# Pinned short products of the ones matrix in TensorE's waits of the norm chains

## The chip, the cores and the metric

The kernel runs on one core of one Trainium2 chip. The metric is the device time of one execution in microseconds (us); the median of several runs is given. Beside it there is one profiled execution, whose trace gives a start and a duration for each instruction on TensorE (PE; its weight loads stand apart as PEld), VectorE (DVE), ScalarE (ACT), GpSimd (POOL) and the DMA queues, and the clock that TensorE was granted, as a share of full speed.

## The reference

One inference step of a two-layer backbone on 256 tokens of width 2048: 128 context tokens and 128 latent tokens share all weights. Every layer is a mixer (layer 0: differential attention beside RWKV-7; layer 1: a Conformer convolution) followed by a gated MLP. Ahead of each of the four blocks stands an RMS norm with adaptive scale and shift; inside the Conformer block there is a layer norm besides.

```python
def rmsnorm(x, g, eps=RMS_EPS):
    xf = x.astype(F32)
    y = xf * lax.rsqrt(jnp.mean(xf * xf, axis=-1, keepdims=True) + eps)
    return (y * g.astype(F32)).astype(x.dtype)
...
    for l in range(DEPTH):
        ...
        hs = rmsnorm(xs, norm_g[l, 0]) * (1.0 + sc1s) + sh1s
        # layer 0: ms = ab_mixer(hs, ...)     layer 1: ms = conformer_conv(hs, ...)
        xs = xs + g1s * ms
        hs = rmsnorm(xs, norm_g[l, 1]) * (1.0 + sc2s) + sh2s
        xs = xs + g2s * conv_ffn(hs, w_up[l], w_ffn_dw[l], w_down[l])
...
def conformer_conv(h, w_pw1, w_dw, b_dw, cln_g, cln_b, w_pw2):
    u = h @ w_pw1
    u = u[..., :D_CONV] * jax.nn.sigmoid(u[..., D_CONV:])
    u = dwconv(u, w_dw) + b_dw
    u = jax.nn.silu(layernorm(u, cln_g, cln_b))
    return u @ w_pw2
```

The six adaptive vectors of a layer (`sc1`, `sh1`, `g1`, `sc2`, `sh2`, `g2`) come from a product of SiLU of the conditioning with a 2048 x 12288 matrix, `w_ada`. All data is float32.

## The kernel before

Activations lie transposed: channels on the 128 partitions, the 256 tokens (two streams of 128) along the free axis, in 16 slices of the width, called kt. A large product (`gemm`) runs over kt and makes three matmuls of 128x256 for each output tile, on values split into a rounded high part and a remainder: high by high (L252), high by low (L254), low by high (L255). Weights come from HBM into `raw` tiles (seven of them), ACT rounds them (L192), DVE or POOL takes the remainder (L194), into four `wbt` buffers. With `tail=4` the last four kt of a product run tile by tile (L268 to L270), so that the tiles of the last group end one after the other. The residual and its squares follow each tile on DVE and ACT (L666, L509, L511).

Between two stages stands a norm chain. `rstd_tok` makes the sums of squares of each token with four products of the collected squares with two columns of `ones` (L522); `rstd` takes the root on ACT (L528) and the reciprocal on DVE (L529); `rstd_bcast` puts the two results on a diagonal (`dg`, L534 on ACT and L535 on DVE) and multiplies it with `ones` (L537), which lays the factor on all partitions in PSUM. Then `modulated` makes the next stage's input kt by kt: DVE multiplies (L582), ACT adds the shift and rounds (L585), DVE takes the remainder (L587), and the next product begins with the first kt. This chain runs three times with its sums made on TensorE: ahead of layer 0's MLP, ahead of the Conformer block, ahead of layer 1's MLP. The first norm of all has its sums from ACT and isn't touched; the final one ends the program.

The layer norm of the Conformer block has a chain of its own: sums by products with two columns of `ones` (L1711), a few small DVE and ACT operations (L1715 to L1723), four diagonals (L1728, L1730), one product of 128x512 with `ones` (L1733), and then `hc` kt by kt (L1737 to L541), which the second Conformer product takes.

The products for `w_ada` are spread over the program as fill: `ada_pe` makes them on TensorE (L421), `ada_vec` makes them on DVE (L446) and ends with eight short products (L454). Both collect in one PSUM tile with the tag `ada`, of which there is a single buffer; DVE turns the result round when a part is done (L460) and adds the bias (L473).

The order on each engine is set by a scheduler, which simulates the program's time line and takes the ready instruction of highest priority; `tc.high_priority` raises it. `tc.keep_in_program_order` pins an instruction to its place among the others that are pinned. The engines themselves run their queues in order.

In the program's text the sums, the diagonal and its product of an RMS norm stand in one place, in `modulated`:

```python
with tc.high_priority(0):
    rs = acc if known else rstd_bcast(rstd_tok(acc))
```

The products that the change adds read the constant tile `ones` twice and write the PSUM tile with the tag `ada`:

```python
psa = ctx.enter_context(tc.tile_pool(name="psa", bufs=1, space=PSUM))
ones = const.tile([P, P], F32, name="ones")
```

Of the kernel before, what the change touches and what calls it, by code (L numbers as in the profile page):

```python
# [10 lines left out]
F32 = mybir.dt.float32  # L11
# [8 lines left out]
P = 128  # L20
# [62 lines left out]
def tile_step(ctx: ExitStack, tc: tile.TileContext, A):  # L83
# [42 lines left out]
    def bank():  # L126
        return psm[0].tile([P, 512], F32, tag="mm", name="mm")
# [21 lines left out]
    def new_hb():  # L149
        return Halves([hbp.tile([P, KT // 2, 2 * TT], F32R, tag="hb", name="hbt") for _ in range(2)])  # L150
# [366 lines left out]
    def rstd_tok(acc):  # L517

        ps = bank()
        for s in range(2):  # L520
            for i, src in enumerate((acc, sq_last[0])):
                pe.matmul(ps[:, 2 * s:2 * s + 2], lhsT=src[:, s * T:(s + 1) * T], rhs=ones[:, 0:2], start=(i == 0),  # L522
                          stop=(i == 1))
        return rstd(ps[:, 0:4])
# [7 lines left out]
    def rstd_bcast(sd):  # L532
        dg = nrm_[0].tile([P, TT], F32, tag="dg", name="dg")
        act.activation(dg[:, T:TT], ident, AF.Copy, scale=sd[:, 2:3])  # L534
        dve.tensor_scalar(out=dg[:, 0:T], in0=ident, scalar1=sd[:, 0:1], scalar2=None, op0=ALU.mult)  # L535
        rs = bank()
        pe.matmul(rs[:, 0:TT], lhsT=ones, rhs=dg, start=True, stop=True)  # L537
        return rs

    def split(dst, src, eng=None):  # L540
        act.activation(dst[:, 0:TT], src, AF.Copy)  # L541
        (eng or dve).tensor_tensor(out=dst[:, TT:2 * TT], in0=src, in1=dst[:, 0:TT].bitcast(F32), op=ALU.subtract)
# [19 lines left out]
    def modulated(x, acc, l, ni, known=False, in_psum=False):  # L562
        sh = "sh1" if ni == 0 else "sh2"

        def gen(hb):
            with tc.high_priority(0):
                rs = acc if known else rstd_bcast(rstd_tok(acc))
            pair = [None]
            for kt in range(KT):
                if not in_psum:  # L570
# [887 lines left out]
    with ExitStack():  # L1458
# [55 lines left out]
        with scoped("nrm1", 2) as nrm_[0]:  # L1514
# [76 lines left out]
            with scoped("cv", 1) as cvp, scoped("cvt", 2) as cvt:  # L1591
# [134 lines left out]
                for i in range(4):  # L1726
                    if i % 2:
                        act.activation(dg[:, i], ident, AF.Copy, scale=va[:, 2 * i:2 * i + 1])  # L1728
                    else:
                        dve.tensor_scalar(out=dg[:, i], in0=ident, scalar1=va[:, 2 * i:2 * i + 1], scalar2=None,  # L1730
                                          op0=ALU.mult)
                pbc = bank()
                pe.matmul(pbc, lhsT=ones, rhs=dg.rearrange("p a t -> p (a t)"), start=True, stop=True)  # L1733
                hc = new_hb()
                for ct in range(KT):
                    t = cvt.tile([P, TT], F32, tag="cg", name="cg")
# [79 lines left out]
```

## Time and profile before

| | |
|---|---|
| median of 3 runs | 2710.97 us (2711.49, 2710.97, 2693.57) |
| the profiled execution | 2685.66 us |
| its span, first to last instruction | 2683.7 us |
| mean granted clock of TensorE | 0.982 |
| PE busy | 2590.8 us, 97% of the span |
| DVE busy | 2010.5 us, 75% |
| ACT busy | 1258.9 us, 47% |

The profile's time axis starts with the first instruction. The stages that matter here: layer 0's mixer ends near 807 us, its MLP runs to 1565, the first half of the Conformer block to 1835, its second half to 1949, and layer 1's MLP to the end. In a row of the time line stand the start and the duration in us, the engine, the line of the kernel, the operation, the tiles written and read, how many alike were merged (x), and in brackets the idle time before it with what ended it. A product of float32 operands is carried out as two matmul instructions, so that x2 is one product of the program. In a row of a table of stretches stand the stretch, its length, each engine's busy time with the number of instructions in brackets, the granted clock (PEclk), the share of DMA time and GB/s.

### The profile page before, as it was taken

To read this page: it belongs to the slowest core of one execution; us is meant where nothing else is said; L and a number is where in the kernel's file an instruction comes from. 1 tells how busy PE (TensorE), PEld (TensorE's weight loads), DVE (VectorE), ACT (ScalarE), POOL (GpSimd) and SP (SyncE) were. 2 spreads that over 40 slices of the span, in tenths; PEclk is the share of its full clock that TensorE was granted. 3 is DMA by queue.
4 is the path that set the end of the run, shared out by engine and by line. 5 is a ranking of instruction groups with operands and counts; after the bars stand their busy time and mean duration, and the time that the engine had idled before them with its cause. 6 is when DMAs were issued, how large, how long until landed. Compare 5 with 4: busy or idle time off the path is not lost.

```text
span 2683.7 us, 60347 instructions
## 1 busy us (share of the span) xinstructions
PE 2590.8 (97%) x24347; PEld 2429.0 (91%) x24347; DVE 2010.5 (75%) x3442; ACT 1258.9 (47%) x2063; POOL 310.7 (12%) x333
## 2 busy tenths in 40 slices
PE   6999998999998999999999989999999999999998
PEld 5898995677998999999999979977989999999998
DVE  3667755766579899888999978985389985566655
ACT  4335544545345444434444454345355453355544
POOL 2000111011100000000000038763300000000000
PEclk9999999999798999999999999999999999999999
DMA  9986666656366888877878857876878876666653
GB/s 301 351 286 191 191 181 238 224 182 222 111 193 190 250 261 256 277 247 249 275 251 265 273 161 229 287 256 205 290 235 278 270 233 194 196 193 193 195 191 118
DMA packets 421368, 616.58 MB, mean 230 GB/s; under 512 B 32437, under 2 KB 291864, under 8 KB 420448
## 3 DMA queue, kind: packets, MB, share of 16 engines
q1 hardware_dynamic: 416688, 600.83, 70.4%
q0 software_dynamic: 3040, 6.57, 0.7%
q10 hardware_dynamic: 1360, 5.33, 0.5%
q8 instruction: 191, 3.13, 0.5%
q14 instruction: 89, 0.73, 0.1%
HBM read 604.75 MB, written 7.86 MB: 228 GB/s over the span
## 4 chain that ended last, share of the span: by engine, by line
PE 83%; DVE 4%; DMA 2%; ACT 1%; issue 1%; SPq 0%; POOL 0%; DVEq 0%; ACTq 0%; POOLq 0%
PE mm L252 23%; PE mm L255 23%; PE mm L254 23%; PE ada L421 3%; DMA raw<-in_w_ada 1%; PE mm L1088 1%; DMA raw<-in_w_up 1%; DVE wbt L194 1%; PE mm L1649 1%; PE mm L1121 1%; PE mm L1125 0%; DVE av L446 0%; PE ada L454 0%; PE mm L1283 0%; PE mm L1292 0%
## 5 line engine op out<-in xcount | busy, mean ns | idle before, releaser
L192 ACT ACTIVATE wbt<-raw 128x1024 fp32r<-128x1024 f32 (+3 forms) x768 | 795.3, 1037 | 1033.1 <-PE mm L254 698.1
L252 PE MATMUL mm<-hbt,wbt 128*128 128x256 f32 x3888 | 1085.0, 282 | 8.5 <-ACT hbt L585 6.4
L194 DVE TENSOR_TENSOR wbt<-raw,wbt 128x1024 fp32r<-128x1024 f32 (+1 forms) x688 | 814.1, 1189 | 359.7 <-ACT wbt L192 349.9
L254 PE MATMUL mm<-hbt,wbt 128*128 128x256 f32 x3888 | 1080.7, 280 | 2.2 <-DVE hbt L587 2.1
L255 PE MATMUL mm<-hbt,wbt 128*128 128x256 f32 x3888 | 1063.1, 280 | 7.5 <-DVE wbt L194 5.4
L252 PEld LDWEIGHTS mm<-hbt,wbt 128*128 128x128 f32 x3888 | 732.7, 189 | 26.5 <-issue 12.5
L254 PEld LDWEIGHTS mm<-hbt,wbt 128*128 128x128 f32 x3888 | 733.8, 189 | 5.9 <-DVE hbt L587 4.4
L255 PEld LDWEIGHTS mm<-hbt,wbt 128*128 128x128 f32 x3888 | 723.3, 189 | 12.3 <-DVE wbt L194 6.7
L254 PE MATMUL mm<-u,wbt 128*128 128x256 f32 x1344 | 371.0, 278 | 0.0
L252 PE MATMUL mm<-u,wbt 128*128 128x256 f32 x1344 | 370.9, 278 | 0.0
L255 PE MATMUL mm<-u,wbt 128*128 128x256 f32 x1344 | 365.7, 278 | 0.0
L446 DVE SCALAR_TENSOR_TENSOR av<-raw,silu_c,av 128x1024 f32<-128x1024 f32 x270 | 337.6, 1279 | 35.3 <-DMA raw<-in_w_ada 35.0
L194 POOL TENSOR_TENSOR wbt<-raw,wbt 128x1024 fp32r<-128x1024 f32 x80 | 194.7, 2440 | 910.0 <-DMA raw<-in_w_pw 805.3
L252 PEld LDWEIGHTS mm<-u,wbt 128*128 128x128 f32 x1344 | 252.2, 188 | 0.4 <-issue 0.4
L254 PEld LDWEIGHTS mm<-u,wbt 128*128 128x128 f32 x1344 | 252.0, 188 | 0.4 <-issue 0.4
L255 PEld LDWEIGHTS mm<-u,wbt 128*128 128x128 f32 x1344 | 249.1, 188 | 0.4 <-issue 0.4
L421 PE MATMUL ada<-raw,silu_c 128*32 128x256 f32 (+2 forms) x2688 | 154.3, 332 | 22.5 <-DMA raw<-in_w_ada 16.6
L1656 DVE SCALAR_TENSOR_TENSOR cu<-mm,vec,cu 128x256 f32<-128x256 f32 x428 | 173.7, 474 | 3.0 <-ACT cu L1640 1.6
L1545 DVE SCALAR_TENSOR_TENSOR cv<-mm,vec,cv 128x254 f32<-128x254 f32 x344 | 147.5, 475 | 12.2 <-ACT cv L1540 12.2
L421 PEld LDWEIGHTS ada<-raw,silu_c 128*32 128x32 f32 x2688 | 68.3, 113 | 74.0 <-issue 26.6
L286 PE MATMUL mm<-hbt,wbt 128*128 128x256 f32 x448 | 131.5, 298 | 0.4 <-ACT hbt L585 0.4
L288 PE MATMUL mm<-hbt,wbt 128*128 128x256 f32 x448 | 126.8, 284 | 0.0
(448 smaller groups left out, 2781.1 us busy)
## 6 DMA issues: line engine op xcount, KB each, us to landing
raw<-in_w_ada SPq DMA_DIRECT2D x384, 512.0 KB, 5.3
raw<-in_w_up SPq DMA_DIRECT2D x688, 256.0 KB, 4.2
raw<-in_w_down SPq DMA_DIRECT2D x168, 512.0 KB, 5.0
raw<-in_w_pw SPq DMA_DIRECT2D x128, 256.0 KB, 4.3
raw<-in_w_in SPq DMA_DIRECT2D x64, 384.0 KB, 5.7
raw<-in_w_in SPq DMA_DIRECT2D x48, 512.0 KB, 3.9
raw<-in_w_out SPq DMA_DIRECT2D x32, 512.0 KB, 3.9
raw<-in_w_pw SPq DMA_DIRECT2D x32, 512.0 KB, 5.4
```

The source lines that it names most:

```text
L192: act.activation(w[:, 0, 0:na * n], v, AF.Copy)
L194: pl.lo(pl.count).tensor_tensor(out=w[:, 1, 0:na * n], in0=v, in1=w[:, 0, 0:na * n].bitcast(F32), op=ALU.subtract)
L252: pe.matmul(ps, lhsT=hi, rhs=r[:, 0:TT], start=(ki == 0 and (nl > 0 or j % 2 == 0)), stop=False, skip_group_check=True)
L254: pe.matmul(ps, lhsT=hi, rhs=r[:, TT:2 * TT], start=False, stop=False, skip_group_check=True)
L255: pe.matmul(ps, lhsT=lo, rhs=r[:, 0:TT], start=False, stop=(ki == nk - 1), skip_group_check=True)
L286: pe.matmul(ps, lhsT=hi, rhs=r[:, 0:TT], start=(ki == 0 and j % 2 == 0), stop=False, skip_group_check=True)
L288: pe.matmul(ps, lhsT=hi, rhs=r[:, TT:2 * TT], start=False, stop=False, skip_group_check=True)
L421: pe.matmul(ps[32 * j:32 * j + 32, 0:nb * 32], lhsT=silu_c[:, kt, :], rhs=rv[:, j], start=(kt == 0), stop=(kt == KT - 1))
L446: dve.scalar_tensor_tensor(out=av[:, s], in0=raw, scalar=sc, in1=av[:, s], op0=ALU.mult, op1=ALU.add)
L1088: pe.matmul(dst_[h][:, s * TT:(s + 1) * TT], lhsT=src[pr, s], rhs=kr[pr, s].rearrange("p a t -> p (a t)"), start=True, stop=True)
L1545: dve.scalar_tensor_tensor(out=o[:, :, a_], in0=v2(ps)[:, :, b_], scalar=w(k, ct), in1=o[:, :, a_], op0=ALU.mult, op1=ALU.add)
L1656: dve.scalar_tensor_tensor(out=o, in0=pads[a](k), scalar=V("w_dw", k * KT + ct), in1=o, op0=ALU.mult, op1=ALU.add)
```

## The change

A new function, `turn_over(n)`, takes a fresh PSUM tile of the tag `ada`, named `idle`, and issues `n` products of `ones` with `ones` (128x128 by 128 columns) into it. Nobody reads the result. Each is pinned in the program's order. In `modulated`, where the sums are made on TensorE, two such products stand ahead of the sums, nine between the sums and the diagonal's product, and six behind that product. In the layer norm of the Conformer block six stand ahead of the product of 128x512 and six behind it. That is 17 in each of three chains and 12 in the fourth, 63 in all, which are 126 instructions.

```diff
+    def turn_over(n):
+
+        ps = psa.tile([P, 256], F32, tag="ada", name="idle")
+        for _ in range(n):
+            tc.keep_in_program_order(pe.matmul(ps[:, 0:P], lhsT=ones, rhs=ones, start=True, stop=True))
+
...
             with tc.high_priority(0):
-                rs = acc if known else rstd_bcast(rstd_tok(acc))
+                if known:
+                    rs = acc
+                else:
+                    turn_over(2)
+                    sd = rstd_tok(acc)
+                    turn_over(9)
+                    rs = rstd_bcast(sd)
+                    turn_over(6)
...
+                turn_over(6)
                 pbc = bank()
                 pe.matmul(pbc, lhsT=ones, rhs=dg.rearrange("p a t -> p (a t)"), start=True, stop=True)
+                turn_over(6)
                 hc = new_hb()
```

The pinned products and the shared PSUM tile also move other instructions. The lines below are the order on an engine as the scheduler left it, with x for equal instructions in a row; after the change the new products are on L544, and lines behind the insertions have larger numbers.

The queue of PE ahead of layer 0's MLP, before: the last products of the mixer's output (`hm`), the four for the sums, the diagonal's, the first of the MLP (`hbt`).

```order
L270 MATMUL mm<-hm,wbt 128x256
L522 MATMUL mm<-ones,acc 128x2
L522 MATMUL mm<-ones,sq 128x2
L522 MATMUL mm<-ones,acc 128x2
L522 MATMUL mm<-ones,sq 128x2
L537 MATMUL mm<-dg,ones 128x256
L252 MATMUL mm<-hbt,wbt 128x256 x2
```

The same place now.

```order
L270 MATMUL mm<-hm,wbt 128x256
L544 MATMUL idle<-ones 128x128 x2
L522 MATMUL mm<-ones,acc 128x2
L522 MATMUL mm<-ones,sq 128x2
L522 MATMUL mm<-ones,acc 128x2
L522 MATMUL mm<-ones,sq 128x2
L544 MATMUL idle<-ones 128x128 x9
L537 MATMUL mm<-dg,ones 128x256
L544 MATMUL idle<-ones 128x128 x6
L252 MATMUL mm<-hbt,wbt 128x256 x2
```

Nothing else moved there on PE: the 2, 9 and 6 new products stand as in the text. Ahead of layer 1's MLP the two stand behind the four sums instead, so that eleven follow each other.

The queue of PE ahead of the Conformer block, before: the last product of the MLP (`u`), eight short products that end a part of `w_ada` (`av`, L454), the sums and the diagonal.

```order
L270 MATMUL mm<-u,wbt 128x256
L454 MATMUL ada<-av,sel 32x256 x8
L522 MATMUL mm<-ones,acc 128x2
L522 MATMUL mm<-ones,sq 128x2
L522 MATMUL mm<-ones,acc 128x2
L522 MATMUL mm<-ones,sq 128x2
L537 MATMUL mm<-dg,ones 128x256
L252 MATMUL mm<-hbt,wbt 128x256
```

The same place now.

```order
L270 MATMUL mm<-u,wbt 128x256
L544 MATMUL idle<-ones 128x128 x2
L522 MATMUL mm<-ones,acc 128x2
L522 MATMUL mm<-ones,sq 128x2
L522 MATMUL mm<-ones,acc 128x2
L522 MATMUL mm<-ones,sq 128x2
L544 MATMUL idle<-ones 128x128 x9
L537 MATMUL mm<-dg,ones 128x256
L544 MATMUL idle<-ones 128x128 x6
L454 MATMUL ada<-av,sel 32x256 x8
L252 MATMUL mm<-hbt,wbt 128x256
```

The eight products L454 went from the start of the gap to its end, ahead of the Conformer's first product; on DVE their L460 and L473 went from ahead of the reciprocal L529 to among the first L582 and L587.

The queue of PE at the layer norm, before: sums (`cu`, `csq`, `accq`), `w_ada` products (`ada`, L421) among and behind them, the product of the diagonals.

```order
L421 MATMUL ada<-raw,silu_c 32x256 x4
L1711 MATMUL mm<-ones,cu 128x2 x2
L1711 MATMUL mm<-ones,csq 128x2 x2
L1711 MATMUL mm<-ones,cu 128x2 x2
L1711 MATMUL mm<-ones,csq 128x2 x2
L1711 MATMUL mm<-ones,accq 128x2 x2
L421 MATMUL ada<-raw,silu_c 32x256 x8
L1733 MATMUL mm<-dg,ones 128x512
L252 MATMUL mm<-hbt,wbt 128x256 x2
```

The same place now; L1724 is the old L1711, and L1747 the old L1733.

```order
L1724 MATMUL mm<-ones,cu 128x2 x2
L1724 MATMUL mm<-ones,csq 128x2 x2
L1724 MATMUL mm<-ones,cu 128x2 x2
L1724 MATMUL mm<-ones,csq 128x2 x2
L1724 MATMUL mm<-ones,accq 128x2 x2
L544 MATMUL idle<-ones 128x128 x6
L1747 MATMUL mm<-dg,ones 128x512
L544 MATMUL idle<-ones 128x128 x6
L421 MATMUL ada<-raw,silu_c 32x256 x16
L252 MATMUL mm<-hbt,wbt 128x256 x2
```

This part of `w_ada` (its PSUM tile now comes after the new products') had 32 of its products ahead of L1733, eight of them between the sums and L1733. Now it has none there: 16 stand behind the second six new ones, ahead of the next product's first matmul, and 16 inside that product.

## The prediction

> **What bounds the kernel now.** I read the page first (its chain of waits, and the granted clock in 40 slices, in tenths), for the engine that sets the span, then a table of stretches around the norm chains, for the clock.
>
> ```profile
> PE 83%; DVE 4%; DMA 2%; ACT 1%; issue 1%; SPq 0%; POOL 0%; DVEq 0%; ACTq 0%; POOLq 0%
> PEclk9999999999798999999999999999999999999999
> ```
>
> The chain of waits is 83% TensorE's, so what PE loses is lost. The clock falls only for short times. Four of these follow the norm chains (ahead of layer 0's MLP, of the Conformer block, in its layer norm, ahead of layer 1's MLP; A, B, C and D below):
>
> ```profile
> 809.70:819.80 10.10, 6.66 (x25) 5.59 (x26) 7.45 (x25) 4.75 (x15) 0.00 (x0) 0.50 0.35 106
> 1570.80:1581.00 10.20, 7.22 (x24) 5.55 (x25) 7.68 (x22) 3.13 (x10) 1.13 (x1) 0.50 0.34 105
> 1843.90:1847.30 3.40, 3.40 (x18) 3.40 (x17) 3.33 (x10) 3.27 (x9) 1.18 (x2) 0.50 0.00 0
> 1953.10:1963.35 10.25, 7.77 (x31) 6.75 (x32) 8.79 (x34) 5.90 (x16) 0.00 (x0) 0.50 0.88 283
> ```
>
> After the length, the columns are busy PE, PEld, DVE, ACT, POOL, then the clock: 0.50 for 34 us in all. Between drop and return lie about 10.2 or 3.4 us, and 1570.8 - 809.7 = 761.1 = 223 x 3.413: the clock changes at the ends of fixed windows of 3.41 us. Windows at whose end it fell, and one (1564.00) at whose end it stayed:
>
> ```profile
> 806.30:809.70 3.40, 1.26 (x12) 1.06 (x10) 3.27 (x10) 2.83 (x5) 0.00 (x0) 0.99 0.82 260
> 850.65:854.05 3.40, 0.92 (x7) 0.92 (x8) 3.40 (x7) 0.84 (x2) 0.00 (x0) 0.99 0.64 188
> 1564.00:1567.40 3.40, 1.72 (x23) 0.93 (x21) 2.93 (x5) 3.40 (x7) 2.68 (x2) 1.00 0.12 39
> 1567.40:1570.80 3.40, 1.19 (x8) 1.04 (x8) 2.87 (x5) 2.17 (x8) 3.40 (x2) 1.00 0.49 153
> 1833.70:1837.10 3.40, 2.15 (x22) 1.58 (x21) 1.22 (x7) 1.00 (x4) 0.00 (x0) 0.99 0.89 331
> 1949.75:1953.15 3.40, 0.76 (x6) 0.67 (x6) 2.02 (x3) 1.21 (x2) 0.22 (x1) 0.99 0.81 244
> ```
>
> It fell with PE busy 22 to 37% of a window and stayed at 51%. It also fell at 63% (1833.70), where most of the busy time was L1711, products with two columns: these seem to count for little. So a wait matters by its share of a window, not by its length.
>
> **The change part by part.** 63 products are added. One costs, at full clock, what the nearest float32 products of 128 columns take from start to start, and at half clock at most twice that:
>
> ```profile
> 240.76 0.38 PE L826 MATMUL mm<-aT,kv 128*128 128x128 f32 x2
> 240.98 0.39 PE L827 MATMUL mm<-aT,cv 128*128 128x128 f32 x2
> ```
>
> 0.22 us, so 0.43 at half clock: 63 are 14 us of PE, two are 0.44, six 1.3 or 2.6, nine 2.0 or 3.9. They are free while the wait they fill is longer. A cold large matmul costs more, by these rows:
>
> ```profile
> 817.00:819.80 2.80, 2.80 (x13) 2.80 (x14) 2.80 (x12) 1.63 (x6) 0.00 (x0) 0.50 0.00 0
> 1964.00:1970.00 6.00, 6.00 (x55) 6.00 (x54) 6.00 (x17) 4.48 (x11) 0.00 (x0) 1.00 0.40 108
> 1957.60:1963.30 5.70, 5.70 (x26) 5.70 (x27) 5.70 (x23) 3.61 (x10) 0.00 (x0) 0.50 0.79 254
> ```
>
> 2.80/13 = 0.215 us against 6.00/55 = 0.11: 0.10 us each.
>
> *Chain A:*
>
> ```profile
> 807.29 0.28 PE L270 MATMUL mm<-hm,wbt 128*128 128x256 f32 x1
> 810.68 0.56 PE L522 MATMUL mm<-ones,acc 128*128 128x2 f32 x2 [3.12 <-DVE acc L511]
> 811.96 0.57 PE L522 MATMUL mm<-ones,sq 128*128 128x2 f32 x2
> 813.52 1.22 PE L537 MATMUL mm<-dg,ones 128*128 128x256 f32 x2 [1.00 <-ACT dg L534]
> 817.00 0.58 PE L254 MATMUL mm<-hbt,wbt 128*128 128x256 f32 x1 [0.29 <-DVE hbt L587]
> ```
>
> The first two wait for nothing, so they run at once behind L270 and end near 807.85; 2.83 us of the wait remain, since L522 needs DVE's sums. The sums end near 812.4 at half clock, 811.6 at full. The nine are now ahead of L537 in the queue, and behind L537 stand all of L582, L585, L587 and the MLP. Full clock: the nine end at 813.5 and L537 starts where it did, 0.6 shorter (half of 1.22), and 13 large matmuls save 1.3: -1.9. Half clock: the nine end at 812.4 + 3.9 = 816.3, 2.8 late; L537 by then at full clock gives 0.6 back and the large ones 1.3: +0.9. A wait of 2.83 in 3.41 leaves a whole window 17% at worst; to stay above half in both windows its edge has to fall well inside the wait. I take the drop: **+0.9**.
>
> *Chain B:*
>
> ```profile
> 1564.65 1.07 PE L454 MATMUL ada<-av,sel 128*32 128x256 f32 x16
> 1567.57 0.35 PE L522 MATMUL mm<-ones,acc 128*128 128x2 f32 x2 [1.84 <-DVE acc L511]
> 1569.42 0.36 PE L522 MATMUL mm<-ones,sq 128*128 128x2 f32 x2
> 1572.15 1.19 PE L537 MATMUL mm<-dg,ones 128*128 128x256 f32 x2 [2.37 <-DVE dg L535]
> PE mm L252 <- ACT hbt L585: 4.1, 5, 1.5
> ```
>
> The last row (PE's waits, 1575 to 1610 us: total, times, longest) says that PE waits for its input here: cold matmuls cost nothing, only a later L537 does. L454 filled the window that stayed at 51%; it leaves, two products of 0.44 replace its 1.07, and the window falls to about a third, so I take a drop one window earlier. The sums, stretched a little at half clock, end near 1570.0, the nine at 1570.0 + 3.9 = 1573.9, 1.75 late, and L537 gives 0.6 back: +1.15. On DVE the moved L460 and L473 now stand among the L582 that PE waits for:
>
> ```profile
> 1567.34 0.44 DVE L460 STREAM_TRANSPOSE atr<-ada 128x256 f32<-128x256 f32 x1
> 1567.82 1.84 DVE L473 TENSOR_TENSOR adaT<-atr,vec 128x16 f32<-128x16 f32 x1
> 1570.12 0.18 DVE L529 RECIPROCAL sd<-sd 128x4 f32<-128x4 f32 x1 [0.46 <-ACT sd L528]
> ```
>
> L473, on 16 columns, took 1.84 here; between 0 and that I take 0.2, as L529 on four columns took 0.18 two us later: +0.6 with L460. Weighing a warm B (-0.6 + 0.6 = 0) a little, **+1.5**; at worst 1.15 + 2.28 = +3.4.
>
> *Chain C:*
>
> ```profile
> 1834.62 0.59 PE L1711 MATMUL mm<-ones,accq 128*128 128x2 f32 x4
> 1836.29 0.69 ACT L1728 ACTIVATE dg<-table,va 128x128 f32<-128x128 f32 x2 [0.24 <-DVE va L1722]
> 1837.50 1.08 PE L421 MATMUL ada<-raw,silu_c 128*32 128x256 f32 x8 [0.69 <-DMA raw<-in_w_ada]
> 1838.51 2.08 PE L1733 MATMUL mm<-dg,ones 128*128 128x512 f32 x2
> 1842.64 0.51 PE L252 MATMUL mm<-hbt,wbt 128*128 128x256 f32 x2 [2.05 <-ACT hbt L541]
> ```
>
> The diagonals are ready at 1836.98, but L1733 starts at 1838.51: `w_ada` products that waited for DMA stood ahead of it. Now six new ones stand there, done after 1.3 of the 1.75 us at full clock. From the last L1711 (1835.2) to L252 were 7.4 us, with useful work, at full clock, of 1.1 (eight L421 products; four are x8, 1.08 at half clock) and 1.0 (L1733, half of 2.08): 5.3 lost. Now L1733 starts at 1.75, then come its 1.0, the six (1.3) and 16 L421 products (2.2): L252 at 6.25, less 2.2 and 1.0: 3.05 lost. Its input is no later: L1733's end at 2.75 and the 2.05 of wait behind it give 4.8. That saves 2.25, and the 17 cold matmuls behind, 0.10 each, 1.7: -3.9. But the L421 among the sums are gone: 28 two-column instructions, 3.1 us at 0.11 each (four in 0.59 would be 4.1), follow each other, and by the 63% row such a window can fall. Half of them cold cost 1.5, the six 0.85 more than their room (2.6 for 1.75): -1.6. I take **-2.0**.
>
> *Chain D:*
>
> ```profile
> 1950.14 0.36 PE L522 MATMUL mm<-ones,sq 128*128 128x2 f32 x2
> 1950.49 0.44 DVE L460 STREAM_TRANSPOSE atr<-ada 128x256 f32<-128x256 f32 x1
> 1954.12 1.22 PE L537 MATMUL mm<-dg,ones 128*128 128x256 f32 x2 [3.62 <-ACT dg L534]
> ```
>
> Here all eleven stand behind the sums and wait for L460 (the tile `ada`): 1950.93 to 1953.35 at full clock, ahead of L537. The window that held 22% (to 1953.15) gets 2.2 us more and stays. L537 is 0.6 shorter, and 26 large matmuls (1957.60 to 1963.30) save 2.6: **-3.2**, kept if DVE follows.
>
> Sum: 0.9 + 1.5 - 2.0 - 3.2 = -2.8, on the profiled execution's 2685.66: 2682.9. The median of the runs is 25 above that execution, for a reason that its trace can't show; against it the same step gives 2711.0 - 2.8 = 2708.
>
> **A rule against the rows.** When the clock fell at 1570.80, PE's last waits had been of 1.84 us and less. The Trainium skill, "TensorE: Matmul & The Clock Gate", section "HAM oscillation", says "no PE-idle gaps >~3.4µs" as the rule for a clock that stays up. By that rule alone no chain would drop now, and the sum would be rival 1's. This case's rows disagree: the fall at 1570.80, and the one at 854.05, whose window had 0.92 us busy and so no more than 2.5 without work. The windows of 3413 ns that the page gives, free-running, agree with the 3.41 here.
>
> **The rivals.**
>
> 1. *Every chain stays warm.* The longest wait left is 2.83 us, and an edge may fall within it. -1.9 + 0 - 3.9 - 3.2 = -9.0: 2702. Against it: the window from 850.65, which fell with less idle time than that. Chance 0.2.
> 2. *Slower: cold new products hold L537 up, and the clock does not come back for it.* Place: the nine or eleven behind the sums; they decide from the point where 0.43 each exceeds the wait for the diagonal (1.0 in A, 2.4 in B, 3.6 in D, in L537's brackets). A +2.8 (DVE's chain, with no gain), B +2.3 (1.75 + 0.6), D +1.5 (1950.93 + 4.7 = 1955.6), C 0: +6.6, so 2718. For it: two columns count little, so the sums give the window nothing. Chance 0.15.
> 3. *The time is won and waited for again.* In A's stage PE later waits for weights (first row below, 822 to 920 us: total, times, longest), and in D's DVE has no idle time (6.00 of 6.00 at 1964.00). The second row is the smaller of the only two that D's stage has, 1956 to 2670 us, both in its first two us:
>
> ```profile
> PE mm L255 <- DVE wbt L194: 3.0, 1, 3.0
> PE mm L254 <- DVE hbt L587: 0.3, 1, 0.3
> ```
>
>    Then C's and D's gains shrink to the losses of A and B: 0, 2711. Against it is the second row: D's stage has no later wait. Chance 0.2.
>
> The forecast has 0.45.
>
> **How the numbers follow.** By mechanism the cases span -9 to +6.6 us. The runs before spread wider, 2693.57 to 2711.49, and the profiled execution lies at 2685.66; the median can come from either end. The low end: the profiled one less the forecast's 2.8, 2683, a little beyond it for rival 1; the high end: 2711.5 plus 6.6, 2718. One per cent is 27 us, about what a measurement of this kernel tells from no change. No case reaches it alone; a median at the low end with rival 1 or the forecast does (0.08); a slower planned order that the rows don't show might (0.03).
>
> **What would show it.** Right: half clock gone after 1953 and shorter after 1843; L1747 starting under 2 us behind the last L1724; a drop still at A and B, with the nine at 0.43 each and L537 late. Wrong: 0.22 each in A (rival 1), half clock behind L537 in D (rival 2), new waits of L255 on L194 or of L252 on L585 in D's stage (rival 3). A gain above 10 us would mean that idle time outside the four chains moved.

## The result, and the profile after

| | before | after |
|---|---|---|
| median of 17 runs each | 2693.57 us (2683.76 to 2714.09) | 2715.44 us (2710.39 to 2724.35) |
| ratio, 95% interval | | 1.0069 [1.0048, 1.0089] |
| the profiled execution | 2685.66 us | 2721.01 us |
| its span | 2683.7 us | 2719.2 us |
| mean granted clock | 0.982 | 0.984 |

The change made the kernel slower by 0.7%, though the mean granted clock went up. On the page of the kernel after, the chain of waits and the clock in 40 slices look much as before, with fewer dips of the clock:

```profile
PE 82%; DVE 4%; DMA 2%; ACT 1%; issue 1%; SPq 0%; POOL 0%; DVEq 0%; ACTq 0%; POOLq 0%
PEclk9999999999899999999999999999999999999999
```

So the loss is TensorE's own time, and most of it isn't the clock. I lined the two traces up at marks that both have: the last large matmul ahead of a chain, and the n-th large matmul behind it.

| from ... to ... | before | after | difference |
|---|---|---|---|
| start to the last L270 ahead of A | 807.3 | 813.3 | +6.0 |
| A: last L270 to the 100th large matmul behind | 22.6 | 22.6 | 0.0 |
| from there to the last L270 ahead of B | 734.5 | 733.8 | -0.7 |
| B: to the 100th behind | 31.6 | 32.1 | +0.5 |
| from there to the last L270 ahead of D (C is in it) | 349.6 | 347.8 | -1.8 |
| D: to the 100th behind | 25.9 | 26.4 | +0.5 |
| 100th to 300th behind D | 22.7 | 30.8 | +8.1 |
| 300th behind D to the 1000th | 79.3 | 83.9 | +4.5 |
| from there to the end of the span | 610.2 | 628.6 | +18.4 |

The first row lies ahead of the first new product: two executions differ by that much there. The chains themselves all but cancel. The loss is in layer 1's MLP, and most of it hundreds of microseconds behind the last new product. Two pieces of it can be seen.

*First piece: the spacing.* Stretches of 460 us near the end of both kernels, where TensorE never waits, first the kernel before, then the kernel after (the columns of a table of stretches are those told ahead of the prediction):

```profile
2190.00:2650.00 460.00, 460.00 (x4061) 460.00 (x4060) 276.66 (x382) 217.91 (x283) 0.00 (x0) 1.00 0.62 192
```

```profile
2210.00:2670.00 460.00, 460.00 (x3908) 460.00 (x3907) 264.36 (x359) 207.65 (x269) 0.00 (x0) 1.00 0.60 187
```

Both are busy throughout, both at a granted clock of 1.00, with the same work in the queue; but one starts 4061 matmuls and the other 3908. That is 460/4061 = 113.3 ns and 460/3908 = 117.7 ns from start to start. From the starts themselves the two values are 113.33 and 117.78 ns, 4.44 ns apart, and nothing between them is held for long. I call them short and long; a train is a row of large matmuls that follow each other without a break, and a stop is what breaks it. A train can keep its value for hundreds of microseconds, and where the value changes, other products or a wait nearly always interrupt the matmuls there. In the kernel before this last happened at a stop of four `w_ada` products:

```profile
2181.21 0.64 PE L454 MATMUL ada<-av,sel 128*32 128x256 f32 x8
2184.34 0.64 PE L454 MATMUL ada<-av,sel 128*32 128x256 f32 x8
```

Before: long from 2076 us up to the second of these stops, short from there to the end, 4,218 matmuls without a break. After: the same two stops stand at 2197.97 and 2201.01; between them the train is short, behind the second it is long to the end. Over the whole program the kernel before has 6,163 short and 11,239 long spacings, the kernel after 1,080 and 16,356. In layer 1's MLP alone there are 5,206 short ones before and 109 after: 5,097 x 4.44 ns = 22.6 us of the 35.5 between the two profiled spans.

*Second piece: new waits behind D.* TensorE's waits in the kernel after, 1963 to 2090 us (total, times, longest):

```profile
PE mm L255 <- DVE wbt L194: 4.1, 2, 3.8
PE mm L254 <- DVE hbt L600: 0.9, 2, 0.6
PE mm L252 <- ACT wbt L192: 0.9, 1, 0.9
```

The kernel before had only 1.5 us there, all in D itself. The clock follows: 20 us in which the kernel after starts 120 matmuls, at a clock that fell once more (a mean of 0.92 over 20 us is what one window of some 3.4 us at half clock gives):

```profile
1985.00:2005.00 20.00, 15.86 (x120) 15.33 (x119) 17.84 (x29) 9.32 (x14) 0.00 (x0) 0.92 0.73 212
```

### The profile page after: what moved, and what is told of

It is laid out like the page before. It is cut to its first block, busy times and chain, and to the rows that moved or that the text cites. A ratio compares the mean times of both kernels' runs of the same rounds, so it can differ in the third digit from the quotient of the medians.

```text
span 2719.2 us, 60565 instructions
## 1 busy us (share of the span) xinstructions
PE 2631.4 (97%) x24473; PEld 2467.9 (91%) x24473; DVE 2008.6 (74%) x3442; ACT 1259.8 (46%) x2063; POOL 311.1 (11%) x333
## 4 chain that ended last, share of the span: by engine, by line
PE 82%; DVE 4%; DMA 2%; ACT 1%; issue 1%; SPq 0%; POOL 0%; DVEq 0%; ACTq 0%; POOLq 0%
PE mm L252 23%; PE mm L254 22%; PE mm L255 22%; PE ada L421 3%; PE mm L1101 1%; DMA raw<-in_w_ada 1%; DVE wbt L194 1%; DMA raw<-in_w_up 1%; PE mm L1662 1%; DVE av L446 1%; PE idle L544 1%; PE mm L1134 1%; ACT wbt L192 0%; PE mm L1138 0%; PE mm L1322 0%
## 5 line engine op out<-in xcount | busy, mean ns | idle before, releaser
L192 ACT ACTIVATE wbt<-raw 128x1024 fp32r<-128x1024 f32 (+3 forms) x768 | 794.9, 1036 | 1054.7 <-PE mm L254 711.3
L194 DVE TENSOR_TENSOR wbt<-raw,wbt 128x1024 fp32r<-128x1024 f32 (+1 forms) x688 | 812.5, 1188 | 382.6 <-ACT wbt L192 376.3
L252 PE MATMUL mm<-hbt,wbt 128*128 128x256 f32 x3888 | 1083.6, 282 | 5.1 <-ACT hbt L598 3.4
L255 PE MATMUL mm<-hbt,wbt 128*128 128x256 f32 x3888 | 1066.5, 280 | 9.8 <-DVE wbt L194 7.6
L252 PEld LDWEIGHTS mm<-hbt,wbt 128*128 128x128 f32 x3888 | 728.1, 188 | 21.1 <-issue 12.5
L255 PEld LDWEIGHTS mm<-hbt,wbt 128*128 128x128 f32 x3888 | 721.6, 188 | 16.3 <-DVE wbt L194 10.1
L252 PE MATMUL mm<-u,wbt 128*128 128x256 f32 x1344 | 372.9, 279 | 0.0
L255 PE MATMUL mm<-u,wbt 128*128 128x256 f32 x1344 | 367.7, 279 | 0.0
L194 POOL TENSOR_TENSOR wbt<-raw,wbt 128x1024 fp32r<-128x1024 f32 x80 | 194.3, 2436 | 914.7 <-DVE acc L511 804.1
L252 PEld LDWEIGHTS mm<-u,wbt 128*128 128x128 f32 x1344 | 252.3, 188 | 0.4 <-issue 0.4
L255 PEld LDWEIGHTS mm<-u,wbt 128*128 128x128 f32 x1344 | 248.6, 187 | 0.4 <-DVE u L1573 0.4
L421 PE MATMUL ada<-raw,silu_c 128*32 128x256 f32 (+2 forms) x2688 | 155.3, 334 | 22.3 <-DMA raw<-in_w_ada 16.3
L421 PEld LDWEIGHTS ada<-raw,silu_c 128*32 128x32 f32 x2688 | 68.8, 114 | 74.4 <-issue 27.5
```

Of the source, the lines that this page charges most:

```text
L192: act.activation(w[:, 0, 0:na * n], v, AF.Copy)
L194: pl.lo(pl.count).tensor_tensor(out=w[:, 1, 0:na * n], in0=v, in1=w[:, 0, 0:na * n].bitcast(F32), op=ALU.subtract)
L252: pe.matmul(ps, lhsT=hi, rhs=r[:, 0:TT], start=(ki == 0 and (nl > 0 or j % 2 == 0)), stop=False, skip_group_check=True)
L255: pe.matmul(ps, lhsT=lo, rhs=r[:, 0:TT], start=False, stop=(ki == nk - 1), skip_group_check=True)
L421: pe.matmul(ps[32 * j:32 * j + 32, 0:nb * 32], lhsT=silu_c[:, kt, :], rhs=rv[:, j], start=(kt == 0), stop=(kt == KT - 1))
```

## The experiments

The theories, as the expectations number them. 1: at each stop of TensorE's stream the spacing is drawn anew, and holds. 2: the order that the change gives to layer 1's MLP makes its matmuls slower in itself. 3: the kind of stop sets the spacing. 4: the chains A to C cost the time. 5, formed later: where the moving operand and the weights lie in SBUF sets which spacings there are. 6: the order of output tiles does.

**Which part of the change: only D, all but D, and one more stop**

```diff
-                else:
+                elif (l, ni) not in PADS:          # D alone: PADS = [(1, 1)]
+                    rs = rstd_bcast(rstd_tok(acc))
+                else:
                     turn_over(2)
```

```diff
                     ada_step()
+                    if (1, "g2") in ada_done:
+                        late[0] += 1
+                        if late[0] == 4:
+                            turn_over(1)           # one more product, behind the last L454
```

> The products of the change only ahead of layer 1's MLP (chain D); elsewhere the order of the kernel before. Theory 2 (the order that D's products give to layer 1's MLP makes its large matmuls slower): spacing 117.8 ns there, 22 us from it and some 6 us from the new waits behind D, so about 2712 to 2718 as the change itself. Theory 1 (drawn at the last stop): the last 4,200 matmuls run at one of the two spacings, so the time is either near 2697 or near 2716, whatever is in D. Theory 4 (the other three chains cost): near the kernel before, within 5 us.

> The change without its products in chain D; layer 1's MLP has the order of the kernel before. Theory 2: spacing 113.3 ns in the last 4,200 matmuls in nearly all executions, time within 4 us of the kernel before. Theory 1: the stop is the same but its instant is another, so the spacing can be either: near the kernel before or 19 us above. Theory 4: the whole loss, 20 us.

> The change, and one more product of ones with ones some 150 matmuls behind the last L454 of layer 1's MLP, where no stop was. Theory 1: the spacing is drawn again there: 4,050 matmuls at 113.3 (18 us below the change, near 2697) or at 117.8 (as the change), and the trace shows the new spacing begin at that product. Theory 2: no difference, 117.8 ns to the end, within 1 us of the change.

| | median, us | ratio to before, 95% interval |
|---|---|---|
| D only | 2716.05 | 1.0069 [1.0033, 1.0105] |
| all but D | 2696.48 | 1.0010 [0.9974, 1.0046] |
| change and one more product | 2716.42 | 1.0086 [1.0059, 1.0114] |

Within what these runs can tell, D alone is the whole loss; theory 4 falls. With D's products all ten timed runs of "D only" lie at 2712 or above; without them six of ten lie at 2686 to 2700 and four at 2707 to 2713. The profiled execution of "all but D" is of the upper group (2707.43 us). Its last 460 us behind the last stop:

```profile
2195.00:2655.00 460.00, 460.00 (x3908) 460.00 (x3907) 264.56 (x361) 207.68 (x270) 0.00 (x0) 1.00 0.60 187
```

From D's product on, TensorE has the same 6,266 matmul instructions in the same order as in the kernel before, and still the spacing is long. So theory 2 doesn't hold as stated: one and the same order ends at either spacing, and 4,218 x 4.44 ns = 18.7 us is the distance between the two groups of times, which the 17 runs of the kernel before show too (2684 to 2697 and 2708 to 2714). But it isn't a fair coin: with D's products no run of 37 came below 2710. The extra stop was long on both sides, which a draw allows; it told nothing apart.

**The spacing by itself**

> A program of its own, which computes nothing of the reference: 140 trains of 24 to 26 large matmuls (128x256, weights loaded for each, as in L252 to L255), and behind each train one stop of ten kinds in a shuffled order, 14 of each: 8, 4 or 1 products of 32 columns as in L454; 1, 2 or 6 products of ones with ones; one product as in L537; four with two columns as in L522; a wait for ACT; a wait for DVE. Theory 1 (the steady spacing is drawn anew at each stop of TensorE's stream and then holds): every train runs at one of two spacings, 113.3 or 117.8 ns, without a change inside it, and for most kinds both occur; a share of about 0.1 to 0.5 at 113.3. Theory 2 (the spacing belongs to the layer's MLP, to its weights' arrival or to the other engines' load): with no other engine at work all trains run at one spacing. Theory 3 (a kind of stop sets it): each kind gives one of the two in all 14.

This program is a loop of trains like L252 to L255 with their weights, each behind a stop; but for the two kinds of wait no other engine works. Every train, whatever its stop, settled within some six matmuls at a third value, 120.0 ns. Theory 3 falls for this program, and theory 1 as well: nothing was drawn. What differs from the kernel must be something else. In this program the weights and the moving operand both begin at 128 bytes modulo 256 (the remainder of the start address in a partition, divided by 256); in the kernel at 224 and 32. These places are those that the programs were laid out for; the profile holds no addresses. The next one varied that:

```python
pe.matmul(ps, lhsT=wb[:, w, ow + k * P:ow + (k + 1) * P], rhs=hb[:, c:c + TT], ...)   # ow, c: offsets
```

> Again a program of its own that computes nothing of the reference: trains of 48 to 54 large matmuls, each behind one stop of four products as in L454, with the weights and the moving operand begun at offsets of 0 to 384 bytes (multiples of 32) in their tiles, three trains for each pair; 40 pairs with the order of output tiles as in the kernel (three matmuls to one tile, four tiles in turn), two with all into one tile. In the run of the ten kinds of stop every train had settled at 120.0 ns whatever the stop, a third value. Theory 5 (where the two operands lie in SBUF sets which steady spacings there are): the pairs differ, with 113.3 for some and 117.8 or 120.0 for others, the three trains of a pair alike. Theory 6 (all matmuls into one output tile made the 120.0): 120.0 for the two pairs with one tile, 113.3 or 117.8 for the 40. Theory 1 (drawn at each stop): the three trains of one pair differ. If all are at 120.0, it is something that this program lacks (waits between the engines, or their load).

Some of the 42 cases (three trains each; the mean spacing ahead of a train's end, in ns, worked out from the starts of the matmuls; the distance is from the weights' begin to the moving operand's, modulo 256 bytes):

```
distance   0 (8 pairs, and the 2 with one output tile): 120.0 at the end of all trains
distance  96 (4 pairs):  120.0 in all
distance 128 (7 pairs):  118.4 to 118.9
distance  64 (6 pairs):  117.8 in 17 trains, 113.3 in 1
distance 192 (5 pairs):  117.8 in 6 trains, 113.3 in 9
```

Theory 5: yes. Theory 6: no, one output tile or four in turn made no difference. Within a distance of 64 (the kernel's) or 192 bytes both values occur for one and the same pair, so there is a draw as well, and the place weights it.

> Once more a program of its own that computes nothing of the reference: trains of 30 to 36 large matmuls, four for each case; the moving operand begun 0 to 252 bytes behind the weights (the distance taken modulo 256), in steps of 8 bytes behind one stop of four products as in L454, and distances of 64 and 192 bytes at three places of the weights behind that stop, eight such products, and a wait for DVE. In the run with 42 pairs of offsets the distance alone set what a train could settle at: 0 and 96 bytes 120.0 ns, 64 bytes (the kernel's) 117.8 in 17 of 18 trains and 113.3 in one, 192 bytes 113.3 in 9 of 15. Theory 5 (the distance of the operands in SBUF): the same shares here whatever the stop, 113.3 in about a tenth at 64 bytes and in over a half at 192 bytes. Theory 3 (the kind of stop decides at these distances): q8 and the wait differ from the four products at one and the same distance.

Distances in steps of 8 bytes gave spacings from 113.3 to some 122 ns (the mean of a train's last 12). At 64 bytes 6 of 40 trains were short, at 192 bytes 26 of 40: there 11 of 16 behind four products, 8 of 12 behind eight and 7 of 12 behind a wait for DVE, so the kind of stop is no clear cause. One distance, 112 bytes, was short in four of four.

**The kernel with its weights elsewhere**

The weights' tile moved by 128 bytes, so that the distance becomes 192:

```diff
-        wbt[0] = wbp.tile([P, WB, 2, 1024], F32R, tag="wb", name="wbt")
+        wide = wbp.tile([P, WB * 2048 + 32], F32R, tag="wb", name="wbt")
+        wbt[0] = wide[:, 0:WB * 2048].rearrange("p (b h x) -> p b h x", b=WB, h=2)
```

> The kernel before with the weights' tile 128 bytes lower in SBUF, nothing else changed, same order on every engine: the moving operands then begin 192 bytes behind the weights modulo 256, where they were 64 behind. Theory 5: over a half of the stretches between two stops at 113.3 ns where now a tenth is; some 11,000 of the large matmuls were at 117.8, so 4.4 ns x 11,000 x 0.5 = 25 us at the most, 5 to 25 us below the kernel before, and the share at 113.3 in the trace over 0.5. Theory 1 (a draw that the addresses do not weight): within 5 us of the kernel before. Theory 2 (the order of layer 1's MLP): no difference.

> The change with the weights' tile 128 bytes lower, nothing else. Theory 5: the last 4,200 matmuls at 113.3 ns in most executions, the loss of 19 us gone, and the time within 5 us of the kernel before with the same shift, or below it by the chains' gain of about 3. Theory 2: 117.8 ns in layer 1's MLP whatever the addresses, so 20 us above the shifted kernel before.

The kernel before with this one shift: 2669.65 us, ratio 0.9896 [0.9865, 0.9928]; the change with it: 2680.41 us, 0.9928 [0.9901, 0.9956]. In the traces 11,787 and 13,743 of some 17,900 spacings are short. The last 460 us of the shifted kernel before are short again (4061), and of the shifted change too. Theory 5 stands; but the change stays 10.8 us behind the kernel before with the same shift, where it was 22, and not within the 5 us expected, though more of its spacings are short. So something besides the spacing costs time.

By 48 bytes instead, for the distance of 112 that was short four times of four:

> The kernel before with the weights' tile 48 bytes lower in SBUF, nothing else, same order: the moving operands then begin 112 bytes behind the weights modulo 256. In the run of distances this one gave 113.3 ns in four trains of four. Theory 5 (the distance sets which spacings there are): nearly all large matmuls at 113.3; with 11,200 of 17,900 at 117.8 in the trace of the kernel before, 4.44 ns x 11,200 = 50 us at the most, less where TensorE waits for weights: 2640 to 2665. If the whole kernel's other loads matter more than the distance: between this and the kernel before, with both spacings in the trace.

> The change with the weights' tile 48 bytes lower, nothing else. Theory 5: with one spacing left, what remains between this and the shifted kernel before is the chains and the waits behind D: by the two traces +0.5 us up to D's first large matmul and +6 for new waits for w_ada and weights behind it, so 0 to 8 us above the shifted kernel before. Theory 2 (the order behind D makes the large matmuls slower in itself): about 20 us above it. The prediction's sum, without the spacing: 2.8 us below it.

> The change without its products in chain D, with the weights' tile 48 bytes lower. If the new waits behind D are what is left of the loss: 3 to 8 us below the shifted change, and within 3 us of the shifted kernel before. If the chains A to C cost: above the shifted kernel before by as much as the shifted change. The prediction's sum for A to C is +0.4 us.

A miss: 2735.13 us (1.0139 [1.0102, 1.0176]), 2746.69 (1.0181 [1.0148, 1.0214]) and 2737.91 (1.0142 [1.0108, 1.0176]). The trace of the first, near its end:

```profile
2210.00:2670.00 460.00, 460.00 (x3836) 460.00 (x3835) 261.39 (x357) 205.26 (x266) 0.00 (x0) 1.00 0.59 183
```

460/3836 = 119.9 ns; elsewhere in it trains run at 116.7. So the distance alone isn't the rule: in the kernel the moving operand begins at 32 bytes modulo 256 and the weights then at 176, in the program of trains they were at 240 and 128. The three still tell something. Their mean spacings are near each other, 119.11, 119.24 and 119.02 ns (0.13 ns on 17,900 matmuls is 2.3 us), and yet the change is 11.6 us behind the shifted kernel before, "all but D" only 2.8.

> A program of its own that computes nothing of the reference: the moving operand begins at 32 bytes modulo 256, as in the kernel, and the weights at each of the 64 multiples of 4 bytes modulo 256; five trains of 30 to 36 large matmuls for each place, four behind a stop of four products as in L454, one behind a wait for DVE. Theory 5 in its wider form (the places of both operands, not their distance alone, set what spacings there are): weights at 224 bytes, the place in the kernel, give 117.8 and seldom 113.3; at 96 bytes (128 lower) 113.3 in about half; at 176 bytes (48 lower) 116.7 and 120.0, as the shifted kernels had; and some place may give 113.3 or less in all five. Theory 5 in its first form (the distance alone): 113.3 in all five at 176 bytes.

This time the moving operand stood where it does in the kernel, and the weights at each of 64 places. Three of its trains, as rows of the time line (L112 is the large matmul; the weights at 108, 224 and 176 bytes):

```profile
571.90 3.68 PE L112 MATMUL mm<-hbt,wbt 128*128 128x256 f32 x31
...
549.83 3.34 PE L112 MATMUL mm<-hbt,wbt 128*128 128x256 f32 x27
...
576.42 3.52 PE L112 MATMUL mm<-hbt,wbt 128*128 128x256 f32 x28
```

The last matmul's own 0.28 off, 3.40/30 = 113.3 ns, 3.06/26 = 117.7 and 3.24/27 = 120.0. Weights at 224 bytes, where the kernel has them, gave long four times and short once; at 176, 120.0 in all five, as the miss had it; at 108, short in all five. At 96 it was short in all five too, where about half was expected: in the kernel moved by 128 bytes, which has its weights there, a third of the spacings were long. So five trains don't tell the share that a place gives in the kernel. Over the 64 places the spacing went from 113.3 to 123.3 ns. Places 4 bytes apart can differ by 7 ns, and I see no rule in them.

**One spacing left: the change without the draw.** The weights at 108 bytes, 116 lower than before:

```diff
+        wide = wbp.tile([P, WB * 2048 + 32], F32R, tag="wb", name="wbt")
+        wbt[0] = wide[:, 3:3 + WB * 2048].rearrange("p (b h x) -> p b h x", b=WB, h=2)
```

and, for the last of the four runs, `cnt[0] > 16` in the `fill2` of layer 1's MLP (the step from which it takes up `w_ada`) made `cnt[0] > 32`.

> The kernel before with the weights' tile 116 bytes lower in SBUF (108 modulo 256, the moving operands at 32), nothing else, same order. In the run of the 64 places this one gave 113.3 ns in five trains of five. Theory 5 in its wider form: nearly all large matmuls at 113.3 in the kernel too; 11,200 of them were at 117.8 in the trace of the kernel before, so 4.44 ns x 11,200 = 50 us at the most, less where TensorE waits for weights: 2640 to 2665. If weights that begin at a multiple of 4 bytes alone slow ACT and DVE, which write them: their groups show longer means, and the gain is smaller or a loss.

> The change with the weights' tile 116 bytes lower, nothing else. If one spacing is left, what stands between this and the shifted kernel before is the change without the spacing. The prediction's sum: 2.8 us below it. By the traces (+0.5 us up to D's first large matmul, 5 to 6 us of new waits for weights behind D, 1.4 gained there on cold matmuls): 3 to 8 us above it. If the order behind D slows the large matmuls in itself: 20 us above it.

> The change without its products in chain D, with the weights' tile 116 bytes lower. If chain D alone loses: within 2 us of the shifted kernel before, and 3 to 8 us below the shifted change. The prediction's sum for A to C: +0.4 us.

> The change with the weights' tile 116 bytes lower, and w_ada's last parts begun 16 steps later in layer 1's MLP, so that VectorE has none of their products (L446) in the first 50 us behind chain D. If the new waits for weights behind D come from VectorE, which cannot finish the norm's slices, the weights' remainders and w_ada's products in that time: the waits of L255 for L194 there are gone, 4 to 6 us below the shifted change. If they come from the loads or from ACT: no difference.

| weights at 108 bytes | median, us | ratio to the kernel before, 95% interval | short spacings |
|---|---|---|---|
| kernel before | 2654.47 | 0.9838 [0.9803, 0.9873] | 16,740 of 17,885 |
| the change | 2665.63 | 0.9873 [0.9840, 0.9907] | 16,768 of 17,877 |
| all but D | 2655.56 | 0.9846 [0.9809, 0.9883] | 16,798 of 17,880 |
| the change, `w_ada` later | 2657.98 | 0.9850 [0.9818, 0.9883] | 16,667 of 17,877 |

The kernel before with its weights 116 bytes lower beats both kernels, by 1.6% the one and by some 2.2% the other. ACT and DVE write the weights there as fast as before (ACT's mean is 1038 ns for 1037; DVE's group on the page of the kernel before, then of the shifted one; the second number is the mean in ns):

```profile
L194 DVE TENSOR_TENSOR wbt<-raw,wbt 128x1024 fp32r<-128x1024 f32 (+1 forms) x688 | 814.1, 1189 | 359.7 <-ACT wbt L192 349.9
```

```profile
L195 DVE TENSOR_TENSOR wbt<-raw,wbt 128x1024 fp32r<-128x1024 f32 (+1 forms) x688 | 814.4, 1190 | 338.1 <-ACT wbt L193 330.4
```

With one spacing in both, the change costs 2665.63 - 2654.47 = 11.2 us by the medians; without D it costs 1.1. So about 11 of the 22 us between the medians are the change itself, most of them D's, and the rest is the spacing. These are six runs each, with up to 15 us between the lowest and the highest, so the 11.2 and the 1.1 are good to several us. The traces give D less: from the last large matmul ahead of D to the end of the span are 741.0 us in the shifted change, 735.0 without D's products and 734.7 in the shifted kernel before, so 6 us. The other 6 us by which the traced change is behind lie ahead of D (8.0 lost from A to B, 3.9 won from C to D). "All but D" has the same order of instructions there and reaches D 0.8 us ahead of the shifted kernel before, so this is no part of D's cost; what it is stays open.

D's part is seen in the 200 matmuls from the 100th to the 300th behind it, first in the shifted change, then with `w_ada` later:

```profile
1946.40:1976.20 29.80, 25.45 (x202) 24.66 (x202) 28.62 (x48) 15.51 (x27) 0.00 (x0) 0.94 0.77 229
```

```profile
1944.50:1967.20 22.70, 22.70 (x202) 22.70 (x202) 19.41 (x42) 15.77 (x29) 0.00 (x0) 1.00 0.61 185
```

TensorE stands still for 4.35 us of the first and loses the clock for one window more (0.94 of 29.80 us); in the second it never waits. VectorE is busy for 28.62 of 29.80 us in the first, for 19.41 of 22.70 in the second. TensorE's waits of the 129 us behind D's product name VectorE, first in the shifted change:

```profile
PE mm L256 <- DVE wbt L195: 3.9, 3, 3.0
PE mm L255 <- DVE hbt L601: 1.2, 2, 0.6
PE mm L253 <- ACT wbt L193: 0.9, 1, 0.9
```

then with `w_ada` later:

```profile
PE mm L255 <- DVE hbt L601: 1.2, 2, 0.6
PE mm L256 <- DVE wbt L195: 1.0, 2, 0.5
```

The waits for weights go from 3.9 to 1.0, and the time falls by 7.7 us by the medians, by 5.1 behind D in the two traces. So they came through VectorE, which in that stretch makes the norm's 16 slices, the weights' remainders and `w_ada`'s products one after the other. What the row of the kernel after shows of it is the wait for `w_ada`'s data in the middle of that queue:

```profile
1996.93 1.28 DVE L446 SCALAR_TENSOR_TENSOR av<-raw,silu_c,av 128x1024 f32<-128x1024 f32 x1 [2.16 <-DMA raw<-in_w_ada]
```

While VectorE waits 2.16 us for that load, the remainders (L194) behind it, already needed, wait too. Of the 3.8 us that TensorE waited there, up to 2.2 are thus the load's and the rest VectorE's work ahead of the remainder (in the shifted change, 1.18 of 3.05 us). The run with `w_ada` later takes away its products and its loads at once, so it doesn't part the two; what was expected of it (no difference, if the loads were the cause) overlooked that. All six kernels with D's products and the old start of `w_ada` have this: 28.3 to 30.8 us from the 100th to the 300th large matmul, against 22.7 to 24.0 in the kernels without them, and 22.7 with `w_ada` later.

*Open.* What decides at a stop between the two spacings that a place allows, and why no run with D's products and the old place of the weights was below 2710 (the three traced all ended long) where most runs of the kernel before were, wasn't settled. Why the places of the operands matter wasn't tried beyond moving them.

## Why the prediction was wrong

It forecast a median of 2708 and no measurable change, from -2.8 us for four chains. Its bound for no change, 1%, holds for the ratio, 1.0069; but the interval excludes 1, and the sign is the other one. The measured 2715.44 lies inside its range of 2683 to 2718, and that is luck: the base of three runs was 17 us above the median of 17 (2693.57), and the high end was made for a late L537, which isn't where the time went. Two steps failed: the sum took the spacing outside the chains as fixed, and chain D was to keep the clock up and to win 3.2 us that VectorE would follow.

**The base.** "For a reason that its trace can't show" the median of three runs lay 25 us above the profiled execution. By the two groups of run times most of it is the spacing drawn at the last stop, 18.7 us; no trace of a slower run of the kernel before was kept, but the one of "all but D" (2707.43 us), which has the same order there, shows it. The trace of before would have shown two spacings at one clock, in two stretches of layer 1's MLP:

```profile
1965.00:2070.00 105.00, 105.00 (x929) 105.00 (x929) 103.20 (x146) 57.59 (x88) 0.00 (x0) 1.00 0.81 253
2080.00:2180.00 100.00, 100.00 (x851) 100.00 (x851) 97.81 (x120) 48.06 (x68) 0.00 (x0) 1.00 0.85 269
```

929 matmuls in 105 us are 113.0 ns each, 851 in 100 us 117.5. I counted one stretch alone ("6.00/55 = 0.11") and took it for the price. This is the step that failed for half of the loss: the sum took the spacing outside the chains as fixed, and no rival had it move. What the runs showed in its place are two spacings, 113.33 and 117.78 ns, and 22.6 us between the two traces from them.

**Chain A**, +0.9: measured 0.0 up to the 100th matmul. The drop came and the nine ran at half clock, as forecast:

```profile
813.41 0.61 PE L544 MATMUL idle<-ones 128*128 128x128 f32 x4
816.16 0.35 PE L522 MATMUL mm<-ones,acc 128*128 128x2 f32 x2 [2.15 <-DVE acc L511]
...
817.05 3.88 PE L544 MATMUL idle<-ones 128*128 128x128 f32 x18
820.77 0.60 PE L537 MATMUL mm<-dg,ones 128*128 128x256 f32 x2
```

(820.77 - 817.05)/9 = 0.41 each. They held L537 up by 1.25 us against its place behind the last L270 (7.48 for 6.23), not by 2.8: the sums themselves ran at full clock, since the drop came later. **Chain B**, +1.5: the first L252 was 1.51 later against the last L270, and 1.0 of that came back by the 100th matmul.

**Chain C**, -2.0: measured -0.3 from the last two-column product to the first L252 (7.68 to 7.37). The part told as the risk was the case: the sums, now without L421 among them, let the clock fall, and the six took 2.70 us in a room of 1.75.

**Chain D**, -3.2: here the mechanism failed twice. "The window that held 22% gets 2.2 us more and stays": it held 1.75 us of 3.41, 51%, and fell; the eleven took 4.5 us instead of 2.4, and L537 came 11.30 behind the last L270 where it had come 8.49. Windows of the kernel after at whose end the clock fell (C, D), and the one behind D:

```profile
1834.48:1837.89 3.41, 3.41 (x30) 3.33 (x30) 0.84 (x2) 0.81 (x2) 0.00 (x0) 0.99 0.02 8
...
1953.95:1957.36 3.41, 1.75 (x11) 1.48 (x12) 1.65 (x3) 2.22 (x4) 0.22 (x1) 0.99 0.95 313
1957.36:1960.67 3.31, 3.31 (x17) 3.31 (x17) 1.53 (x3) 0.46 (x2) 0.00 (x0) 0.50 1.09 350
```

The first shows how little two-column products count: TensorE is busy for the whole window by the profile, all but its first 0.5 us with them, and the clock falls. In the second the last 1.0 us holds new products, and the rest of the 1.75 is two-column sums. The rule read from the rows ("stayed at 51%") was too coarse. The Trainium skill's rule, in "TensorE: Matmul & The Clock Gate", section "HAM oscillation" (no gaps above some 3.4 us), would have kept the clock up in both windows; these rows disagree with it, as those of before did. Still, by the products behind L537 the clock was back at the first large matmul, and the gain on cold ones came in: from the first L252 to the 100th matmul 13.3 us for 15.0. With the late L537 that leaves D 0.5 us slower at the 100th matmul, where 3.2 were to be won.

The second failure is the condition "kept if DVE follows". It didn't. Rival 3 had the mechanism (won time is waited for again, L255 on L194), but priced it at nothing beyond the gain, and took "D's stage has no later wait" as evidence against it. As I read it, the kernel before had no later wait because its cold matmuls left VectorE, busy for 103 of the 105 us in the row above, the time that it needed; with the change TensorE, counted from the first L252, reached the 100th matmul 1.7 us sooner, and from there to the 300th it lost 8.1 us, more than it had won. Two waits for L194 and one for L192 are 5.0 of these; the longest, 3.8 us, let the clock fall for one window more, which is 1.6 (0.08 of the 20 us at 1985); the long spacing there is 0.9. How much of the waits the earlier TensorE made and how much the other planned order behind D, the runs don't part.

**Rivals 1 and 2** didn't hold: no chain stayed warm (half clock once in each, for one window, some 14 us in all where the rows of the prediction had 34), and L537 was held up in A, B and D by 1.25, 1.2 and 2.8 us, but each delay was mostly regained on warm matmuls.

## What to carry to other kernels

Before small waits are priced, count the starts of the steady instruction in several equal stretches of the trace: where the counts differ at one clock, a few nanoseconds times thousands outweigh every wait that the change is about, and two groups in the run times are a sign of it. Where TensorE's loads and moving data come from SBUF, try the place of one of the two tiles; a small program of trains showed good and bad places in one run, the place itself, not only the distance, has to be copied from the kernel, and the whole kernel has to be run with it. Before a gain on the engine that bounds the kernel is counted, see whether the engine that feeds it has time to spare just behind that point: here VectorE was all but full there, and taking `w_ada`'s products and loads out of its queue was worth more than the clock.

## What the runs showed of the hardware that I had not expected

- One and the same float32r matmul of 128x256 with its weight load repeats at 113.3 to 123.3 ns at full granted clock, by where in SBUF its two operands begin (steps of 4 bytes matter). The Trainium skill, "TensorE: Matmul & The Clock Gate", section "Step-by-step: what each phase is for", says that loading the next tile's weights doesn't steal SBUF read bandwidth from the running matmul. These runs show a dependence on the two places that a reader of that sentence wouldn't expect; whether reading bandwidth is its cause wasn't tried.
- Some places allow two spacings. Which of them a train takes was settled at its start, within a few matmuls, and could then hold for thousands (4,218 at 113.33 ns in the kernel before).
- A window of 3.41 us in which TensorE was busy throughout by the profile, all but its first 0.5 us with products of two columns, ended with the clock at half.
